# Spreading the latent convolution's blocks among the context's taps in the second half, with one load of its taps a block ahead and four output tiles for the scan

## The chip, the cores and the metric

One core of one Trainium2 chip runs the whole program. The metric is the device time of one execution in microseconds (us), the median of several runs; lower is better.

## The reference: what is computed

One layer of a hybrid backbone runs over two groups of tokens: 256 context tokens and 2048 latent tokens (a grid of 32 rows and 64 columns), 1024 channels wide.

```python
h = rms_norm(x, g_pre) * (1 + scale) + shift
z, xbc, dt_raw, ga, gb, gsil = split(h @ w_in)          # 5664 columns
y_ssd  = bidirectional chunked scan of silu(conv5(xbc)), dt_raw  # chunks of 128 tokens
y_conf = silu(layer_norm(depthwise_conv31(ga * sigmoid(gb)))) * silu(gsil)
out = concat(y_ssd * silu(z), y_conf) @ w_out
return x + gate * rms_norm(out, g_post)                  # and the final states of the context
```

`depthwise_conv31` has 31 taps for each channel. For the context it runs along the 256 tokens; for the latent tokens it runs down the 32 rows of the grid, for each column apart. Those two convolutions are what the change moves about.

## The kernel before, in words

All matrix products are made in pairs of rounded and remainder parts: a weight is split into `wh` and `wl`, the input into `hh` and `hl`, and a product is three matmuls (`wh*hh`, `wh*hl`, `wl*hh`; lines 461 to 463). The tokens are 18 tiles of 128; the first half of the program takes the projections of 10 tiles, the second half (token blocks 3 and 4, 512 tokens each) those of the other 8. The split weights of the first half are kept in DRAM, and the second half loads them again (`load_w`, lines 418 and 419: 512 KB for `wh`, 512 KB for `wl`, three buffers each, asked for three units ahead by `next_w`).

After its `xbc` columns the second half runs through `post(1, 5)`: eight `gab_unit` (each 96 matmuls of 128x512: `gb` and `ga` for two token blocks), then eight `silu_unit` for `z` (48 matmuls each), then those for `gsil`. Into this stream, line by line, `interleave` sets the side work as `merge` counts it out:

- **The scan of tiles 9 to 17** (`scan`, `pass_a`, line 730). A tile loads its inputs `xT` (one buffer) and `bc`, and eight `lb` tiles, rows of running sums spread over all partitions (line 746, issued by ScalarE's queue). GpSimd masks an `lb` (line 758), ScalarE takes its exponential (766), VectorE combines the two directions (770, 771), and TensorE multiplies (`py` 802, `po` 809, `pst` 815 to 817). `skip` (line 836) begins the output tile `yg` from `xT`, and `close` (841) ends it and stores it to `yp`. `yg` has two buffers.
- **The extra work** (line 1061): four context convolutions (`ctx_conv`, line 668: 31 steps on VectorE in 13 pieces) and eight latent convolutions (`lat_conv`, line 701: 6 pieces each), one for each 128 channels, in the order lat, ctx, lat, lat, ctx, lat, and so on: a latent convolution stands right after another, or 13 pieces after it.

A latent convolution is 256 small matmuls (32x64, line 718) of a matrix of taps `kt` with the inputs `cx`. `lat_load` (line 691) brings both in: four loads of 128 KB for the taps `kd` (line 698: 32 partitions each, overlapping stretches of the padded taps) and four of 256 KB for `cx` (line 699: 1024 pieces of 256 bytes each). ScalarE reverses `kd` into `kt` (line 707); from then on `kd` is free. The results pass through two banks of PSUM at a time; VectorE brings them into `cvv` (line 722; one buffer), and four transfers store them (line 727, again in pieces of 256 bytes). `kd` and `cx` have two buffers, `kt` one. A convolution asks for the next one's loads when the next one's inputs are complete (`gl_done`); if not, the next one loads them itself at its own beginning.

All transfers but the `lb` go through the queue of SyncE (SP), which takes them strictly in order: one that has to wait for its buffer or its data holds all behind it. The builder gives each transfer of SP and ScalarE one of eight completion counters in turn, so that a transfer also waits for the one that had this counter last. The PSUM has three banks for the projections (`mm`) and five in turn for all else (`ss`): scan and convolutions share those five.

The order in which each engine takes its instructions is not that of the text. A scheduler in the builder sorts them by a timeline of its own (last lines of the file), so a change of the text moves instructions on every engine. Line numbers below are of this kernel; behind line 692 they are up to 7 higher in the changed one.

Of the kernel before, what the change touches and what calls it, by code (L numbers as in the profile page):

```python
# [8 lines left out]
F32 = mybir.dt.float32  # L9
# [8 lines left out]
P = 128  # L18
# [30 lines left out]
def merge(a, na, b, nb):  # L49

    steps, x, y = [], 0, 0
    for _ in range(na + nb):
        if y * na >= x * nb and x < na or y >= nb:
            steps.append(a)
            x += 1
        else:
            steps.append(b)
            y += 1
    return steps


def take(gen, n):
    for _ in range(n):
        yield next(gen, None)
# [20 lines left out]
def backbone_kernel(ctx, tc, xa, xt_in, cols, rows, wconv, conf_b, gp_row, bg_row, state0, w_mod, w_dt, w_in, w_out,  # L85
# [3 lines left out]
    V, S, T, DMA = (InOrder(tc, e) for e in (nc.vector, nc.scalar, nc.tensor, nc.sync))  # L89
# [30 lines left out]
    def place(i):  # L120

        return (0, i) if i < HT[0] else (1, i - HT[0])
# [66 lines left out]
    pa = ph_a.enter_context(tc.tile_pool(name="pa", bufs=1))  # L189
# [423 lines left out]
    def gab_unit(half, j, hb):  # L613
        wb = next_w()
        wa = next_w()
        gl_done.discard(j)
        for b in ORDER[half]:
            BN, o = BNS[b], TOK[b]
            pg = bank("mm", f"gb{half}_{j}_{b}")
            yield from mm_cm(pg, wb, hb[b])  # L620
            th = ev(f"gth{half}_{j}_{b}")[:, :BN]
            S.activation(th, pg[:, :BN], AF.Tanh, scale=0.5)
            pa_ = bank("mm", f"ga{half}_{j}_{b}")
            yield from mm_cm(pa_, wa, hb[b])
            V.scalar_tensor_tensor(th, th, 1.0, pa_[:, :BN], ADD, MUL)
            DMA.dma_start(GL[j][:, o:o + BN], th)
        if half:
            gl_done.add(j)

    def silu_unit(half, c0, dst, j, hb, order=None):  # L630
        w = next_w()
        for b in order or ORDER[half]:
            BN, o = BNS[b], TOK[b] - half * HT[0] * P
            ps = bank("mm", f"sp{half}_{c0}_{j}_{b}")
            yield from mm_cm(ps, w, hb[b])
            th = ev(f"sth{half}_{c0}_{j}_{b}")[:, :BN]
            S.activation(th, ps[:, :BN], AF.Tanh, scale=0.5)  # L637
            V.scalar_tensor_tensor(th, th, 1.0, ps[:, :BN], ADD, MUL)  # L638
            DMA.dma_start(dst[half][j * P:(j + 1) * P, o:o + BN], th)


    def gate_rows():
        acc = [slab(f"gacc{a}") for a in range(2)]
        for k in range(KT):
            wg = big(f"wg{k}")
            DMA.dma_start(wg, w_mod[k * P:(k + 1) * P, 2 * D:3 * D])
            for a in range(2):
                if k == 0:
                    V.here("tensor_scalar", acc[a][:, :D], wg, sc[:, a, 0:1], None, MUL)
                else:  # L650
                    V.here("scalar_tensor_tensor", acc[a][:, :D], wg, sc[:, a, k:k + 1], acc[a][:, :D], MUL, ADD)
            yield
        br = [slab("bgr0")[0:1, :D], slab("bgr1")[0:1, :D]]
        DMA.dma_start(br[0], bg_row)
        DMA.dma_start(br[1], gp_row)
        for a in range(2):
            for n in range(2):
                ps = bank("ss", f"gp{a}{n}")
                cs = slice(n * 512, (n + 1) * 512)
                T.matmul(ps[0:1, :], ones[:, 0:1], acc[a][:, cs], start=True, stop=True)  # L660
                o = big(f"gr{a}{n}")[0:1, :512]
                V.tensor_tensor(o, ps[0:1, :], br[0][:, cs], ADD)
                V.tensor_tensor(o, o, br[1][:, cs], MUL)
                DMA.dma_start(GGD[a:a + 1, cs], o)
        yield


    def ctx_conv(j, tile):
        g = tile(f"cg{j}")
        G.memset(g[:, 0:15], 0.0)  # L670
        G.memset(g[:, 271:286], 0.0)
        DMA.dma_start(g[:, 15:271], GL[j][:, 0:256])
        yield
        acc = g[:, 512:768]
        w0 = C_CONFW + j * CW
        V.here("tensor_scalar", acc, g[:, 0:256], cv[:, w0:w0 + 1], cfb2[:, j:j + 1], MUL, ADD)
        for t in range(1, CW):
            V.here("scalar_tensor_tensor", acc, g[:, t:t + 256], cv[:, w0 + t:w0 + t + 1], acc, MUL, ADD)
            if t % 3 == 0:
                yield  # L680
        o = g[:, 768:1024]
        S.mul(o, acc, 0.5)
        DMA.dma_start(CV[j * P:(j + 1) * P, 0:256], o)
        yield
# [6 lines left out]
    def lat_load(j, lp):  # L691
        kd = lp.tile([P, 32, 32], F32, tag="kd", name=f"kd{j}", bufs=2)
        x = lp.tile([P, 32, 64], F32, tag="cx", name=f"cx{j}", bufs=2)
        lat_in[j] = kd, x
        for a in range(4):
            rs = slice(a * 32, (a + 1) * 32)
            src = bass.AP(tensor=wconv.tensor, offset=(j * 4 + a) * 64 * 32, ap=[[32, 32], [1, 1024]])
            DMA.dma_start(kd[rs].rearrange("p r g -> p (r g)"), src)
            DMA.dma_start(x[rs], GL[j][:, 256:].rearrange("(g a) (r w) -> a r g w", a=4, w=64)[a])

    def lat_conv(j, lp, cbb, more):
# [28 lines left out]
    def pass_a(i):  # L730
        half, il = place(i)
# [102 lines left out]
        yg = {}  # L834

        def skip(g):
            yg[g] = pa.tile([P, 4, P], F32, tag="yg", name=f"yg{i}{g}", bufs=2)
            V.tensor_tensor(yg[g], xT[:, 4 * g:4 * g + 4, :],
                            cv[:, C_D + 4 * g:C_D + 4 * g + 4].unsqueeze(2).to_broadcast([P, 4, P]), MUL)

# [35 lines left out]
        decay(0, 1)  # L876
        mask(1, 0)
        skip(0)
        load_lb(1, 1)
        yield  # L880
# [37 lines left out]
    def scan(tiles):  # L918

        gens = [pass_a(i) for i in tiles]  # L920
        live, t = [], 0
        while gens or live:
            if gens and t % 7 == 0:
                live.append(gens.pop(0))
            for g in list(live):
                if next(g, 0) == 0:
                    live.remove(g)
            t += 1
            yield


    def interleave(blocks, side, n):
        done = 0
        total = len(side)
        for a, _ in enumerate(blocks):
            want = min(total, -(-total * (a + 1) // n))
            while done < want:
                next(side[done], None)
                done += 1
        while done < total:  # L940
            next(side[done], None)
            done += 1

    def chain(gens):
        for g in gens:
            yield from g

    def run(gen):
        for _ in gen:
            pass  # L950

    def post(half, nb):
        return chain([gab_unit(half, j, hb) for j in range(8)] + [silu_unit(half, Z0, ZS, j, hb) for j in range(8)]
                     + [silu_unit(half, GS0, GS, j, hb) for j in range(nb)])
# [76 lines left out]
    extra = chain([gate_rows()] + [ctx_conv(j, big) for j in range(4)])  # L1031
# [21 lines left out]
    lp = ph_l.enter_context(tc.tile_pool(name="lp", bufs=1, side="right"))  # L1053
# [4 lines left out]
    blocks = post(1, 5)  # L1058
    cg = lambda name: lp.tile([P, D], F32, tag="cg", name=name, bufs=2)
    lat = lambda j: lat_conv(j, lp, cbb, gl_done.__contains__)  # L1060
    extra = chain(f for j in range(4) for f in (lat(2 * j), ctx_conv(j + 4, cg), lat(2 * j + 1)))
    sc_ = scan(range(9, NT))
    run(take(blocks, 24))
    interleave(take(blocks, 24), [sc_] * 4, 24)
    interleave(take(blocks, 344), merge(sc_, 63, extra, 8 * 6 + 4 * 13), 344)
    run(sc_)
    run(extra)
    ph_l.close()
# [107 lines left out]
    def norms(i, yz, nq):  # L1176

        pm = bank("ss", f"pm{i}")
        src = [(c, e, t[1]) for c, e, t in ((0, 4.0 * EPS, yz), (1, EPS, nq)) if t]
        for c, e, t in src:  # L1180
            T.matmul(pm[:, c:c + 1], t, ones[:, 0:1], start=True, stop=True)
        rs = []
        for c, e, t in src:
            ms = p1.tile([P, 1], F32, tag=f"ms{c}", name=f"yms{i}{c}", bufs=2)
            V.tensor_scalar(ms, pm[:, c:c + 1], 1.0 / D, e, MUL, ADD)
            rs.append((c, rstd_of(p1, ms, f"yr{i}{c}")))
        return rs
# [116 lines left out]
    i = order[0]  # L1304
# [21 lines left out]
    for b in range(2):  # L1326
        for m, u in enumerate(last):
            run(take(u, 8))
            if b == 0 and m == 1:
                rs = norms(i, yz, None)  # L1330
# [18 lines left out]
            if b == 1 and m == 0:  # L1349
                rs = norms(i, None, nq)  # L1350
                nq = conf_sqsum(i1, vv[1][0])
            if b == 1 and m == 1:
                n, v = nn[0], vv[0][0]
# [3 lines left out]
            if b == 1 and m == 2:  # L1357
                gs0, v0, n = gs_load(i), v, nn[1]
# [17 lines left out]
    i, nxt, nx2 = order[:3]  # L1376
    banks(i)
    out_part(pso[i], yh, 0, 1)
    rs = norms(nxt, yz, nq)
# [42 lines left out]
    n, n2 = n2, conf_load(order[3])  # L1422
    yh = yhn

    for a, i in enumerate(order[1:], 1):
# [7 lines left out]
        rs = None if last else norms(nxt, yz, nq)  # L1433
# [46 lines left out]
        if a + 3 < NT:  # L1480
            ssd_load(order[a + 3])
            n, n2 = n2, conf_load(order[a + 3])
        else:
            n = n2
# [72 lines left out]
```

## Time and profile before

| What | us |
|---|---|
| Median of 3 runs (1851.51 to 1853.14) | 1852.8 |
| The profiled execution's own time | 1855.05 |
| its span, first to last instruction | 1853.3 |
| TensorE matmul busy in the span | 1793.9 |
| VectorE / ScalarE / GpSimd busy | 1216.5 / 867.1 / 172.2 |
| Mean granted TensorE clock | 0.987 |

The profiled execution took 1.75 us more than its span, and 2.25 us more than the median. The stage with the scan of tiles 9 to 17 and the extra work lies between about 910 and 1300 us. In a table by windows each row gives a stretch, its length, and for each engine the busy time and the count of instructions, then the granted TensorE clock (1.00 is full), the busy share of the 16 DMA engines, and GB/s. In a timeline each row gives the start, the duration (of a merged group: from its first start to its last end), engine, line, operation and tile, and in brackets how long the engine had been idle and what ended that. "SPq" and "ACTq" are the queues that issue transfers.

### The profile page before, as it was taken

The numbers are of one execution on the slowest core, as the hardware profiler recorded it, in microseconds if no ns is written. First come the engines' busy times: TensorE is split into PE (matmuls) and PEld (weight loads), VectorE is DVE, ScalarE is ACT, GpSimd is POOL, SyncE is SP. The second block draws the span as 40 slices with busy tenths as digits, with TensorE's granted clock in tenths as the row PEclk, the third lists the DMA queues.
The fourth block names the chain that finished last, engine by engine and source line by source line (L and its number), as shares of the span: only waits on it lengthen the run. The fifth ranks groups of instructions, "written<-read, shape, count | busy, mean of one in ns | idle before, by whom it ended". The sixth has DMA issues, their size and how long they took to land.

```text
span 1853.3 us, 29884 instructions
## 1 busy us (share of the span) xinstructions
PE 1793.9 (97%) x11167; PEld 1480.5 (80%) x11167; DVE 1216.5 (66%) x1847; ACT 867.1 (47%) x1960; POOL 172.2 (9%) x281
## 2 busy tenths in 40 slices
PE   5999999999999999999999889999999999999998
PEld 2888887888888888888877667777787888888886
DVE  4597857575666762687457375868347878777763
ACT  4747424444455431744235344554245545454441
POOL 1002001011111000100002011110000101111110
PEclk9999999999999999999999889999999999999999
DMA  9656566554786654545697889694977666656632
GB/s 334 215 198 238 204 212 212 190 201 162 261 267 216 222 182 145 178 170 201 195 207 225 176 239 233 229 236 176 290 223 238 194 184 167 172 171 170 185 103 80
DMA packets 304429, 375.22 MB, mean 202 GB/s; under 512 B 84246, under 2 KB 203670, under 8 KB 304284
## 3 DMA queue, kind: packets, MB, share of 16 engines
q1 hardware_dynamic: 283548, 335.56, 58.1%
q10 hardware_dynamic: 20736, 37.76, 7.3%
q8 instruction: 88, 1.44, 0.3%
q14 instruction: 57, 0.47, 0.1%
HBM read 243.66 MB, written 129.59 MB: 201 GB/s over the span
## 4 chain that ended last, share of the span: by engine, by line
PE 87%; DMA 8%; issue 1%; ACT 1%; DVE 1%; SPq 1%; POOL 0%; ACTq 0%; POOLq 0%; DVEq 0%
PE op L81 21%; PE sp L461 6%; PE sp L462 6%; PE sp L463 6%; PE xp L462 5%; PE xp L461 5%; PE xp L463 5%; PE ga L461 3%; PE ga L463 3%; PE ga L462 3%; PE gb L461 3%; PE gb L463 3%; PE gb L462 3%; DMA lb<-lt 3%; PE py L802 2%; PE po L809 2%
## 5 line engine op out<-in xcount | busy, mean ns | idle before, releaser
L766 ACT ACTIVATE lb<-lb,WB 128x128 f32<-128x128 f32 x576 | 184.5, 391 | 162.7 <-POOL lb L758 156.6
L461 PE MATMUL sp<-hh,wh 128*128 128x512 f32 (+1 forms) x640 | 240.0, 375 | 0.0
L463 PE MATMUL sp<-hh,wl 128*128 128x512 f32 (+1 forms) x640 | 237.1, 371 | 0.0
L462 PE MATMUL sp<-hl,wh 128*128 128x512 f32 (+1 forms) x640 | 237.0, 370 | 0.0
L758 POOL TENSOR_SCALAR_AFFINE_SELECT lb<-lb 128x512 f32<-128x512 f32 x144 | 109.1, 761 | 729.9 <-ACT el L755 400.5
L463 PE MATMUL xp<-hh,wl 128*128 128x512 f32 (+1 forms) x456 | 168.0, 368 | 0.0
L462 PE MATMUL xp<-hl,wh 128*128 128x512 f32 (+1 forms) x456 | 167.8, 368 | 0.0
L461 PE MATMUL xp<-hh,wh 128*128 128x512 f32 (+1 forms) x456 | 167.0, 367 | 0.0
L558 DVE SCALAR_TENSOR_TENSOR cva<-raw,cwh,cva 128x1280 f32<-128x1280 f32 (+1 forms) x96 | 141.9, 1487 | 20.4 <-ACT cva L552 18.2
L463 PEld LDWEIGHTS sp<-hh,wl 128*128 128x128 f32 x640 | 121.3, 189 | 21.1
L461 PEld LDWEIGHTS sp<-hh,wh 128*128 128x128 f32 x640 | 121.6, 190 | 20.7 <-issue 0.2
L462 PEld LDWEIGHTS sp<-hl,wh 128*128 128x128 f32 x640 | 121.6, 190 | 20.0
L461 PE MATMUL ga<-hh,wh 128*128 128x512 f32 (+1 forms) x320 | 121.3, 379 | 6.4 <-DMA wh<-whd 5.5
L75 DVE SCALAR_TENSOR_TENSOR cg<-cg,cv 128x256 f32<-128x256 f32 x240 | 123.0, 512 | 3.3
L461 PE MATMUL gb<-hh,wh 128*128 128x512 f32 (+1 forms) x320 | 120.5, 376 | 0.0
L463 PE MATMUL ga<-hh,wl 128*128 128x512 f32 (+1 forms) x320 | 119.2, 373 | 0.5 <-DMA wl<-wld 0.5
L462 PE MATMUL ga<-hl,wh 128*128 128x512 f32 (+1 forms) x320 | 119.4, 373 | 0.0
L463 PE MATMUL gb<-hh,wl 128*128 128x512 f32 (+1 forms) x320 | 119.0, 372 | 0.0
L462 PE MATMUL gb<-hl,wh 128*128 128x512 f32 (+1 forms) x320 | 118.9, 371 | 0.0
L770 DVE TENSOR_TENSOR lb<-lb,lb 128x512 f32<-128x512 f32 x72 | 50.8, 706 | 90.0 <-ACT lb L766 71.7
L638 DVE SCALAR_TENSOR_TENSOR sth<-sth,sp 128x512 f32<-128x512 f32 (+1 forms) x80 | 50.4, 630 | 75.6 <-ACT sth L637 70.7
L755 ACT ACTIVATE el<-lb 64x256 f32<-64x256 f32 x136 | 56.3, 414 | 88.8 <-DMA lb<-lt 71.2
(273 smaller groups left out, 3832.9 us busy)
## 6 DMA issues: line engine op xcount, KB each, us to landing
lb<-lt ACTq DMA_DIRECT2D x144, 256.0 KB, 4.6
wr<-in_w_in SPq DMA_DIRECT2D x88, 256.0 KB, 4.9
whd<-wh SPq DMA_DIRECT2D x44, 512.0 KB, 3.4
wld<-wl SPq DMA_DIRECT2D x44, 512.0 KB, 5.2
wh<-whd SPq DMA_DIRECT2D x44, 512.0 KB, 5.5
wl<-wld SPq DMA_DIRECT2D x44, 512.0 KB, 5.9
xT<-xb SPq DMA_DIRECT2D x18, 512.0 KB, 4.2
yp<-yg SPq DMA_DIRECT2D x36, 256.0 KB, 4.9
```

The costliest lines, as they stand in the source:

```text
L75: return self._tc.keep_in_program_order(getattr(self._eng, name)(*a, **k))
L81: return lambda *a, **k: self._tc.keep_in_program_order(f(*a, **k))
L461: T.matmul(ps[:, :BN], wh[:, k, :], hh[:, k, :], start=(k == 0), stop=False)
L462: T.matmul(ps[:, :BN], wh[:, k, :], hl[:, k, :], start=False, stop=False)
L463: T.matmul(ps[:, :BN], wl[:, k, :], hh[:, k, :], start=False, stop=(k == KT - 1))
L558: V.scalar_tensor_tensor(a[:, :n], raw[:, t:t + n], cwh[:, ct * 5 + t:ct * 5 + t + 1], a[:, :n], MUL, ADD)
L638: V.scalar_tensor_tensor(th, th, 1.0, ps[:, :BN], ADD, MUL)
L755: S.activation(el[g][rs, q:q + 2, :], E[g, hq, 0][rs, j::2, :], AF.Exp)
L758: G.affine_select(E[g, hq, d], E[g, hq, d], pattern=[[0, 4], [sg, P]], compare_op=ALU.is_ge, fill=NEG, base=0, channel_multiplier=-sg)
L766: S.activation(lb[:, h, :], lb[:, h, :], AF.Exp, bias=WB[:, i, c + h:c + h + 1])
L770: V.tensor_tensor(a, a, E[g, hq, 1], ADD)
L802: T.matmul(py[g][j * HD:(j + 1) * HD, q * P:(q + 1) * P], xt[g][:, h * HD:(h + 1) * HD], E[g, hq, 0][:, t, :], start=True, stop=True)
```

## The change

Three things change, all in the second half.

1. **Order of the extra work.** Each context convolution is cut into 7 and 6 pieces, and after each stands one latent convolution: ctx 7, lat, ctx 6, lat. Ahead of all stands one piece that loads the first latent convolution's inputs; the pieces to be merged with the scan are one more.
2. **The taps.** The four loads of `kd` become one with three dimensions on the source's side (4 groups, 32 offsets, 1024 values).
3. **The scan's output tiles.** For tiles of the second half (10 to 17) `yg` comes from the pool of the second half, `lp`, with four buffers; tile 9 keeps the two of `pa`.

```diff
@@ lat_load
+        src = bass.AP(tensor=wconv.tensor, offset=j * 4 * 64 * 32, ap=[[64 * 32, 4], [32, 32], [1, 1024]])
+        DMA.dma_start(kd.rearrange("p r g -> p (r g)"), src)
         for a in range(4):
             rs = slice(a * 32, (a + 1) * 32)
-            src = bass.AP(tensor=wconv.tensor, offset=(j * 4 + a) * 64 * 32, ap=[[32, 32], [1, 1024]])
-            DMA.dma_start(kd[rs].rearrange("p r g -> p (r g)"), src)
             DMA.dma_start(x[rs], GL[j][:, 256:].rearrange("(g a) (r w) -> a r g w", a=4, w=64)[a])
@@ pass_a, skip
-            yg[g] = pa.tile([P, 4, P], F32, tag="yg", name=f"yg{i}{g}", bufs=2)
+            pool, n = (lp, 4) if half else (pa, 2)
+            yg[g] = pool.tile([P, 4, P], F32, tag="yg", name=f"yg{i}{g}", bufs=n)
@@
+    def run_once(f):
+        f()
+        yield
@@ second half
-    extra = chain(f for j in range(4) for f in (lat(2 * j), ctx_conv(j + 4, cg), lat(2 * j + 1)))
+    ctxs = [ctx_conv(j + 4, cg) for j in range(4)]
+    extra = chain([run_once(lambda: lat_load(0, lp))]
+                  + [f for j in range(4) for f in (take(ctxs[j], 7), lat(2 * j), take(ctxs[j], 6), lat(2 * j + 1))])
...
-    interleave(take(blocks, 344), merge(sc_, 63, extra, 8 * 6 + 4 * 13), 344)
+    interleave(take(blocks, 344), merge(sc_, 63, extra, 1 + 8 * 6 + 4 * 13), 344)
```

What the scheduler makes of it is seen at three places.

**SP's queue, around the load of the taps of convolution 4** (`kd4`; `cv` is a store of `cvv`, `wh4256`/`wl4256` are `gb`'s weights of unit 5, `wh3232`/`wl3232` are `ga`'s of unit 5, `cx3` are inputs, `yp`, `st` and `gl` stores). Before:

```order
L698 DMA kd4_10488<-in_wconv 32x1024
L727 DMA cv_78<-cvv1_9400 32x32x64 x2
L418 DMA wh4256_1_9642<-whd25_145 128x1024
L419 DMA wl4256_1_9641<-wld25_189 128x1024
L626 DMA gl3_71<-gth1_3_4_9512 128x512
L727 DMA cv_78<-cvv1_9400 32x32x64 x2
L698 DMA kd4_10488<-in_wconv 32x1024 x3
L699 DMA cx3_9706<-gl3_71 32x32x64 x4
L846 DMA yp11_90<-yg110_9630 128x512
L832 DMA st11_108<-sb110_9965 128x512
L626 DMA gl4_72<-gth1_4_3_9718 128x512
L698 DMA kd5_10795<-in_wconv 32x1024
```

and right behind these:

```order
L727 DMA cv_78<-cvv2_9760 32x32x64 x4
L698 DMA kd5_10795<-in_wconv 32x1024
L735 DMA bc13_10312<-xb1_64 128x4x128
L698 DMA kd5_10795<-in_wconv 32x1024 x2
L418 DMA wh3232_1_9646<-whd17_137 128x1024
L419 DMA wl3232_1_9645<-wld17_181 128x1024
```

Now, from `wh4256` to `wh3232`:

```order
L418 DMA wh4256_1_9567<-whd25_145 128x1024
L419 DMA wl4256_1_9566<-wld25_189 128x1024
L626 DMA gl3_71<-gth1_3_4_9427 128x512
L699 DMA cx3_10018<-gl3_71 32x32x64 x3
L727 DMA cv_78<-cvv1_9451 32x32x64 x4
L699 DMA cx3_10018<-gl3_71 32x32x64
L696 DMA kd4_10535<-in_wconv 128x1x1024
L847 DMA yp11_90<-yg110_9550 128x512
L832 DMA st11_108<-sb110_9817 128x512
L626 DMA gl4_72<-gth1_4_3_9693 128x512
L735 DMA bc13_10290<-xb1_64 128x4x128
L418 DMA wh3232_1_9571<-whd17_137 128x1024
```

Between the two weights' `wl4256` and `wh3232` stood 22 transfers, among them six of two convolutions' stores and seven of two convolutions' taps; now there are 14, with four stores and one load of taps. `kd4`, which waits until ScalarE has reversed `kd2`, stood ahead of the stores of `cvv1` and now stands behind them.

**VectorE, where tile 11's output tiles `yg110` and `yg111` are begun** (`lb` line 770 is the sum of the two directions, lines 821 to 825 carry the state on, 843 and 845 end tile 10's `yg`). Before:

```order
L770 TENSOR_TENSOR lb11000_9313<-lb11000_9313,lb11001_9315 128x512
L770 TENSOR_TENSOR lb11010_9390<-lb11010_9390,lb11011_9392 128x512
L821 TENSOR_TENSOR Sf1_260<-Sf1_260,eTf_252 128x512
L823 TENSOR_TENSOR yo101_9369<-po101_9298,el101_8880 128x512
L825 TENSOR_TENSOR Sf1_260<-Sf1_260,pst1010_9303 128x512
L838 TENSOR_TENSOR yg110_9630<-xT11_9258,cv_214 128x512
L625 SCALAR_TENSOR_TENSOR gth1_3_3_9267<-gth1_3_3_9267,ga1_3_3_9269 128x512
L843 TENSOR_TENSOR yg101_9156<-yg101_9156,py101_9293 128x512
L845 TENSOR_TENSOR yg101_9156<-yg101_9156,yo101_9369 128x512
L770 TENSOR_TENSOR lb11100_9508<-lb11100_9508,lb11101_9510 128x512
L838 TENSOR_TENSOR yg111_9685<-xT11_9258,cv_214 128x512
```

Now:

```order
L791 TENSOR_TENSOR xw1001_9130<-xt100_8900,WS_258 128x512
L839 TENSOR_TENSOR yg110_9550<-xT11_9271,cv_214 128x512
L839 TENSOR_TENSOR yg111_9677<-xT11_9271,cv_214 128x512
L770 TENSOR_TENSOR lb10110_9042<-lb10110_9042,lb10111_9044 128x512
L793 TENSOR_TENSOR xwl1001_9132<-xw1001_9130,xwh1001_9131 128x512
L722 SCALAR_TENSOR_TENSOR cvv0_8933<-cp0_0_8934,cbb_8306 128x8x64
```

Both are begun in the middle of tile 10 instead of at its end, far ahead of tile 10's own `yg101`.

**TensorE, where `ga` of unit 6 begins** (`wh3360` and `wl3360` are its weights, `cp3` the banks of convolution 3). Before:

```order
L718 MATMUL cp3_0_10505<-cx3_9706,kt3_10486 32x64
L718 MATMUL cp3_1_10506<-cx3_9706,kt3_10486 32x64
L461 MATMUL ga1_6_3_10573<-hh3_7102,wh3360_1_10111 128x512
L462 MATMUL ga1_6_3_10573<-hl3_7103,wh3360_1_10111 128x512
L463 MATMUL ga1_6_3_10573<-hh3_7102,wl3360_1_10110 128x512
```

Now:

```order
L718 MATMUL cp3_0_10584<-cx3_10018,kt3_10533 32x64
L718 MATMUL cp3_1_10585<-cx3_10018,kt3_10533 32x64
L461 MATMUL ga1_6_3_10482<-hh3_7102,wh3360_1_9961 128x512
L462 MATMUL ga1_6_3_10482<-hl3_7103,wh3360_1_9961 128x512
L461 MATMUL gb1_6_4_10576<-hh4_7312,wh4384_1_9957 128x512
L462 MATMUL gb1_6_4_10576<-hl4_7313,wh4384_1_9957 128x512
L463 MATMUL gb1_6_4_10576<-hh4_7312,wl4384_1_9956 128x512
```

The last three rows come once more, and only then the third matmul of `ga1_6_3`, the first that needs `wl3360`: six matmuls of the next token block now stand ahead of it, and all but the first two small matmuls of convolution 3 stand behind all of `ga1_6_3`.

Counted in projection matmuls on TensorE, the distance from one latent convolution's first matmul to the next one's was 183, 63, 183, 66, 183, 63, 183, and is now 120, 132, 96, 162, 120, 138, 120.

## The prediction

> **What bounds the kernel now.** I read the page first, for the engine that carries the span.
>
> ```profile
> span 1853.3 us, 29884 instructions
> PE 1793.9 (97%) x11167; PEld 1480.5 (80%) x11167; DVE 1216.5 (66%) x1847; ACT 867.1 (47%) x1960; POOL 172.2 (9%) x281
> ```
>
> TensorE's matmuls fill 97% of the span; no other engine is near that. A change that takes no matmul away can only win where TensorE idles or runs at a lower clock. The table by windows says where that is.
>
> ```profile
> 850.00:900.00 50.00, 50.00 (x222) 41.40 (x221) 38.39 (x30) 17.79 (x19) 0.30 (x3) 1.00 0.55 179
> 950.00:1000.00 50.00, 45.94 (x253) 36.48 (x252) 35.56 (x65) 22.82 (x62) 7.03 (x11) 1.00 0.99 238
> 1000.00:1050.00 50.00, 43.61 (x687) 33.79 (x685) 22.10 (x35) 21.20 (x56) 7.77 (x9) 0.90 0.76 186
> 1050.00:1100.00 50.00, 41.34 (x202) 32.37 (x203) 35.65 (x65) 22.18 (x55) 5.34 (x8) 0.90 0.82 209
> 1100.00:1150.00 50.00, 48.58 (x725) 38.46 (x724) 29.45 (x47) 26.55 (x65) 6.95 (x12) 0.97 0.88 243
> 1150.00:1200.00 50.00, 47.24 (x349) 37.49 (x348) 40.46 (x74) 27.14 (x73) 8.37 (x10) 0.93 0.73 221
> 1200.00:1250.00 50.00, 47.40 (x602) 37.41 (x601) 33.73 (x53) 26.34 (x62) 6.31 (x9) 0.93 0.93 240
> 1250.00:1300.00 50.00, 50.00 (x504) 39.55 (x504) 40.66 (x72) 19.41 (x45) 3.06 (x4) 1.00 0.50 173
> ```
>
> Before and behind the stage TensorE is busy 50.00 of 50.00 at clock 1.00. In the six windows between it idles 4.06 + 6.39 + 8.66 + 1.42 + 2.76 + 2.60 = 25.9 us. Where it works there, the granted clock is lower: busy time times the missing share is 43.61 x 0.10 + 41.34 x 0.10 + 48.58 x 0.03 + 47.24 x 0.07 + 47.40 x 0.07 = 16.6 us. So each idle microsecond costs 16.6 / 25.9 = 0.64 us of clock besides, and 42.5 us is the most that this change can win. The next view is TensorE's waits in that stretch.
>
> ```profile
> PE ga L461 <- DMA wh<-whd: 5.5, 1, 5.5
> PE px L778 <- issue: 5.3, 2, 4.1
> PE cp L718 <- DVE cvv L722: 4.4, 1, 4.4
> PE pst L815 <- DVE cvv L722: 3.5, 1, 3.5
> PE cp L718 <- issue: 2.6, 1, 2.6
> PE pst L815 <- ACT xwh L792: 1.7, 1, 1.7
> PE cp L718 <- ACT sb L831: 1.4, 1, 1.4
> PE px L778 <- PE pb L855: 0.7, 1, 0.7
> PE ga L463 <- DMA wl<-wld: 0.5, 1, 0.5
> PE pst L816 <- DVE xwl L793: 0.4, 1, 0.4
> ```
>
> Two groups. The convolutions' own (`cp`, `pst` behind `cvv`) and the late weights: 5.5 + 4.4 + 3.5 + 2.6 + 1.4 + 0.5 = 17.9 us. The scan's: 5.3 + 1.7 + 0.7 + 0.4 = 8.1 us. How the first group arises is seen in SP's queue, in order of time.
>
> ```profile
> 1021.68 0.34 SPq L698 DMA_DIRECT2D kd<-in_wconv  x1
> 1022.11 0.98 SPq L727 DMA_DIRECT2D cv<-cvv  x2
> 1023.19 1.41 SPq L418 DMA_DIRECT2D wh<-whd  x1
> 1026.67 2.38 SPq L727 DMA_DIRECT2D cv<-cvv  x2
> 1029.09 4.31 SPq L698 DMA_DIRECT2D kd<-in_wconv  x3
> 1033.51 5.32 SPq L699 DMA_DIRECT2D cx<-gl  x4
> ...
> 1053.74 5.39 SPq L727 DMA_DIRECT2D cv<-cvv  x4
> 1062.58 0.37 SPq L418 DMA_DIRECT2D wh<-whd  x1
> ```
>
> The queue sat still until 1021.68, since `kd4` waits for ScalarE to free `kd2`; the stores of `cvv1` stood behind it. Other engines then:
>
> ```profile
> 1030.15 0.33 ACTq L746 DMA_DIRECT2D lb<-lt  x1
> 1030.59 0.62 ACT L792 CAST xwh<-xw 128x512 fp32r<-128x512 f32 x1 [8.52 <-DMA wh<-whd]
> 1034.89 1.29 DVE L722 SCALAR_TENSOR_TENSOR cvv<-cp,cbb 128x512 f32<-128x512 f32 x2 [2.22 <-DMA kd<-in_wconv]
> ```
>
> ScalarE stood for 8.52 us ahead of an `lb` load whose completion counter was still held by the `wh` issued at 1023.19; VectorE could not write `cvv2` before 1034.89, when the late stores of `cvv1` (one buffer) had left it. That is the 4.4. Its followers came late (3.5), and the next pile of taps and stores put `ga`'s weights behind it (5.5).
>
> ```profile
> SPq L698 <- ACT kt L707: 24.2, 2, 14.7
> SPq L733 <- DVE yg L838: 19.1, 5, 6.4
> DVE yg L838 <- DMA yp<-yg: 10.6, 4, 4.2
> ```
>
> These rows sum SP's and VectorE's waits in the stage: 24.2 us for freed taps (once 14.7, the one above), 19.1 us because `xT` waits for `skip`, which itself waited 10.6 us for stores of `yg`. The last view is what transfers take, issue to landing: the first five rows in the stage, the sixth in the first half's scan.
>
> ```profile
> lb<-lt ACTq DMA_DIRECT2D x60, 256.0 KB, 5.2
> wh<-whd SPq DMA_DIRECT2D x21, 512.0 KB, 7.0
> cv<-cvv SPq DMA_DIRECT2D x31, 256.0 KB, 5.3
> xT<-xb SPq DMA_DIRECT2D x8, 512.0 KB, 5.6
> kd<-in_wconv SPq DMA_DIRECT2D x24, 128.0 KB, 4.5
> ...
> lb<-lt ACTq DMA_DIRECT2D x29, 256.0 KB, 4.3
> ```
>
> **The change part by part.** *Spreading.* No matmul, vector step or byte is added or taken. One projection matmul takes 50.00 / 222 = 0.225 us, so the distance between convolutions that were close was 63 x 0.225 = 14.2 us, and is at least 96 x 0.225 = 21.6 us now (scan work not counted). In 14.2 us had to fit: matmuls, VectorE, four stores (5.39 us of issue, 5.3 us to land), and the next convolution's first write of `cvv`. In 21.6 us it fits, and `kd4` has gone behind the stores of `cvv1`, so the 14.7 us wait delays nothing that TensorE asks for next. Ahead of `wh3232` 14 transfers are left of 22. All six waits of the first group hang on this; I let four fifths of the 17.9 go, 14.3 us, and keep a fifth because the bytes stay and the five shared banks still mix scan and convolutions. Bounds: 7.9 (only the two behind `cvv`, 4.4 and 3.5) and 17.9.
>
> *One load of taps for four.* 24 issues fewer in SP's queue: three of them took 4.31 us at 1029.09, when the queue was full. It gains nothing by itself where the queue has slack, and frees three completion counters for each convolution. Its landing is not in this trace: at best as a `wh` of the same 512 KB, 7.0 us; at worst as four quarters one after the other, 4 x 4.5 = 18.0 us. For the convolution either is hidden by 21.6 us of lead. I take 7.0, the row of the same size, and no gain or loss of its own.
> [...]
>
> *Four output tiles.* VectorE's 10.6 us of waits for `yp` and SP's 19.1 us behind them end. What is late next is `xT`: `yg110` is begun soon behind its load, up to 5.6 us of wait for VectorE, hidden because the tile's products come more than 33 projection matmuls (7.4 us) later. This, and fewer counters held, helps the second group; but `px` and `pst` also wait for `lb` tiles, which keep their place, so I let half of 8.1 go, 4.0 us. Bounds: 0 and 8.1.
>
> *What comes new.* The order itself shows `wl3360` late: six matmuls were set ahead of the third of `ga1_6_3`. The scheduler's idea of a transfer knows no full queue, so I expect a wait there, between 0 and the 6.0 (5.5 + 0.5) that the like took before. Since `kd5`, two `cx4` and four stores still stand ahead of `wh3360`, I take 4.0. The first load now precedes the first convolution by a whole block; that is ahead of the first of the quoted windows with a loss, so I take it at nothing.
>
> *The end.* Behind 1250 TensorE is full, so what is saved passes on whole. Convolution 7 now ends 36 matmuls (8.1 us) later; DMA has room there (0.50), and its stores are wanted far later.
>
> *Sum.* Idle: 14.3 + 4.0 - 4.0 = 14.3 us; with clock 14.3 x 1.64 = 23.4 us. The profiled execution took 1855.05, so it would take 1831.6; the median stands 2.25 below it: 1852.8 - 23.4 = 1829.4 us.
>
> [...]
>
> **The rivals.**
> *A, slower: the whole load of taps clogs the queue.* If it lands in 18.0 instead of 7.0 us and what is queued behind it waits along, weights come up to 11.0 us late. `ga`'s weights can be asked for only 48 matmuls (10.8 us) ahead of their need and take 7.0, a slack of 3.8, with scan work somewhat more. Units 3 to 7 each have a load of taps in front: five waits of 6.0, as measured, are 30.0 us, with clock 49.2, against 30.0 (18.3 x 1.64) won: 1852.8 + 19.2 = 1872. It decides from 3.7 us late for each unit on (30.0 / 1.64 / 5). For it: `kd` loads hold counters, and one late weight cost 5.5. Against: in the new order `kd4` stands four rows ahead of `wh3232`, but is issued some 11 us before `wh3232` may be. [...] Chance 0.09.
> *B, little won: the transfers bound the stage.* The bytes are the same: shares 0.99 to 0.93 in the six windows make 255.5 us of 300; in 276.6 us that is 0.92, and at 0.99 TensorE idled 4.06 in 50. `lb` tiles land in 5.2 here against 4.3 in the first half. Then half of the first group, all of the second and a wait of 6.0 stay: (8.95 - 6.0) x 1.64 = 4.8 us won, 1848. Against: from 1100 to 1150 the share was 0.88 with 1.42 idle. Chance 0.20.
> *C, all won*: no wait is left and none is new: 1852.8 - 42.5 = 1810.3. For it: before 900 and behind 1250 TensorE shows what it does when nothing is late. Against: all six waits and the scan's would have to go at once. Chance 0.12 for over 33 us.
> *D, nothing:* the scheduler could sort the text's order away. The distances counted in its order say that it did not; but gain and new waits may cancel. Chance 0.08.
>
> **How the numbers follow.** The forecast, 12 to 33 us won, has 0.51. A measurement of this kernel tells about 0.2%, 3.7 us, from no change. Faster: 0.51 + 0.12 + 0.20 = 0.83; same 0.08 (D); slower 0.09 (A). The range leaves out A, D and the ends of B and C: 1811 (C, nearly all won) to 1849 (B).
>
> **What would show it.** Right: the six windows' idle time near 11 us instead of 25.9 and clocks of 0.95 and over; no `cp` waiting for `cvv`, no `yg` for `yp`, and no long wait of SP for `kt` ahead of `cv`; one wait of `ga` for `wl`. `kd`'s landing, 7 or 18 us, decides on the taps. Wrong: `ga` waiting for weights in several units (A), `lb` landing later than 5.2 and POOL waiting for it as before (B), or the same waits moved behind 1250, where TensorE was full.

## The result, and the profile after

The changed kernel takes 1886.1 us (median of 4 runs, 1881.97 to 1889.72) where the kernel before took 1852.2 on the same chip. The ratio on record is 1.0169, with a 95% interval of 1.0147 to 1.0192; the two medians alone, 34.0 us apart, give 1.018, inside that interval. It is slower by 1.7%; forecast were 1829.4 us and a win. The profiled execution's page begins so:

```profile
span 1881.1 us, 29870 instructions
PE 1802.6 (96%) x11167; PEld 1487.0 (79%) x11167; DVE 1215.6 (65%) x1847; ACT 866.5 (46%) x1960; POOL 168.3 (9%) x281
```

VectorE, ScalarE and GpSimd do the same work in the same time. The span of the profiled execution is 27.8 us longer. The table by windows of the stage, of the changed kernel:

```profile
900.00:950.00 50.00, 48.24 (x238) 39.09 (x236) 17.75 (x32) 8.29 (x12) 0.24 (x4) 1.00 0.63 170
950.00:1000.00 50.00, 42.48 (x450) 33.69 (x450) 31.77 (x53) 21.73 (x54) 5.80 (x8) 0.92 0.70 181
1000.00:1050.00 50.00, 45.84 (x458) 36.26 (x458) 31.15 (x54) 22.55 (x56) 7.39 (x10) 0.91 0.94 238
1050.00:1100.00 50.00, 43.04 (x452) 33.67 (x451) 34.05 (x60) 24.80 (x64) 7.53 (x10) 0.93 0.78 199
1100.00:1150.00 50.00, 45.41 (x474) 35.53 (x473) 27.64 (x46) 22.54 (x56) 6.45 (x11) 0.93 0.88 217
1150.00:1200.00 50.00, 40.47 (x425) 31.40 (x423) 28.89 (x51) 22.57 (x58) 5.32 (x8) 0.90 0.67 191
1200.00:1250.00 50.00, 42.55 (x462) 33.52 (x461) 28.27 (x47) 21.17 (x58) 5.22 (x8) 0.97 0.82 208
1250.00:1300.00 50.00, 44.54 (x455) 35.39 (x456) 36.53 (x65) 27.00 (x67) 6.97 (x9) 0.90 0.72 212
```

and of the kernel before the one row that the prediction did not show:

```profile
900.00:950.00 50.00, 49.49 (x481) 40.27 (x480) 20.22 (x32) 13.61 (x21) 1.09 (x5) 1.00 0.80 203
```

From 900 to 1300 TensorE now idles 400 - 352.6 = 47.4 us, before 0.5 + 25.9 = 26.4: 21.0 more. The missing clock times the busy time is 23.5 us, before 16.6: 6.9 more. Together 27.9, so that these 400 us account for the whole of the longer span. The DMA engines are no busier: a mean share of 0.77 in these eight rows, 0.80 before. TensorE's waits in the stage, of the changed kernel (waited for; us in total, times, longest):

```profile
PE cp L718 <- DVE cvv L722: 10.9, 3, 5.6
PE pst L815 <- DVE yo L823: 7.4, 2, 4.8
PE px L778 <- DVE cvv L722: 5.3, 1, 5.3
PE pst L815 <- ACT xwh L792: 5.3, 1, 5.3
PE ga L461 <- DMA wh<-whd: 4.4, 1, 4.4
PE cp L718 <- ACT sb L831: 4.2, 1, 4.2
PE po L809 <- DVE yo L823: 4.0, 1, 4.0
```

Late weights are one of these seven largest rows. VectorE (`yo`) and ScalarE (`xwh`) were late themselves; three of the four long waits for them lead back to these rows:

```profile
949.56 1.29 DVE L839 TENSOR_TENSOR yg<-xT,cv 128x512 f32<-128x512 f32 x2 [11.27 <-DMA xT<-xb]
998.68 0.62 ACT L792 CAST xwh<-xw 128x512 fp32r<-128x512 f32 x1 [9.82 <-DMA kd<-in_wconv]
1221.74 0.84 ACT L755 ACTIVATE el<-lb 64x256 f32<-64x256 f32 x2 [11.93 <-DMA zs<-sth]
```

In the last two rows ScalarE needs neither taps nor `zs`: ahead of each stands an `lb` load that waits for a completion counter which `kd`, and the `zs` queued behind another `kd`, still held. VectorE's `xT` of the first row was issued late, because in SP's queue `cx` stood ahead of it and waited for a store of `gl` behind a load of taps:

```profile
SPq L699 <- DMA gl<-gth: 6.6, 1, 6.6
```

The chain of waits, of the changed kernel, shows how long transfers take beside a load of taps (start, duration, what):

```profile
988.88 9.28 DMA kd<-in_wconv
...
1099.74 14.69 DMA wh<-whd
...
1206.06 15.24 DMA zs<-sth
```

Around the second of these, SP's queue in the changed kernel:

```profile
1098.11 0.54 SPq L696 DMA_DIRECT2D kd<-in_wconv  x1
1098.76 0.42 SPq L847 DMA_DIRECT2D yp<-yg  x1
1099.27 0.38 SPq L832 DMA_DIRECT2D st<-sb  x1
1099.74 0.54 SPq L418 DMA_DIRECT2D wh<-whd  x1
1100.37 0.60 SPq L419 DMA_DIRECT2D wl<-wld  x1
```

Nothing was held in the queue: five issues in 2.9 us. But the trace also has the time of each step of the completion counters, and there the five read (steps, and when they came):

```
kd  issued 1098.11:  1 step at 1099.07;              4 steps 1109.87 to 1111.49
yp  issued 1098.76: 12 steps 1101.38 to 1102.69;     4 steps 1110.84 to 1112.55
st  issued 1099.27: 12 steps 1102.02 to 1103.14;     4 steps 1111.28 to 1113.18
wh  issued 1099.74: 12 steps 1104.40 to 1105.89;     4 steps 1112.51 to 1114.42
wl  issued 1100.37: 12 steps 1107.10 to 1108.17;     4 steps 1113.82 to 1115.73
```

`kd`'s last step comes 13.4 us after the issue. Of each transfer behind it 12 of the 16 steps have come after 4 to 8 us; the last of the other four comes only after `kd`'s last. Twelve of the sixteen steps of `wh` had come at 1105.89; TensorE stood until 1114.47 for the rest. All eight loads of taps have one step 1.0 to 2.2 us after the issue and then four, the last of them 9.3 to 17.5 us after it. In the kernel before, each of the 32 loads of taps has 16 steps, the last 2.4 to 7.5 us after the issue. Those have 32 as the slowest dimension of both sides, the one load has 4 and 128. No trace here shows the DMA engines one by one: that a late step stands for one of the sixteen engines, and that the one load so runs on four of them, is my reading of these steps.

How many transfers come late can be counted from the same steps. Of those issued from 900 to 1300, the last step came more than 10 us after the issue for these (in brackets how late, us):

```
      before             changed
wh    1 of 23 (10.2)     5 of 21 (12.0 to 14.7)
wl    1 of 23 (10.4)     5 of 21 (13.1 to 15.4)
yp    none of 17         4 of 16 (11.8 to 13.8)
xT    none of 8          1 of 8  (16.1)
```

The rest changed little: the median `wh` needed 5.7 us before and 6.4 now. The table of issues is no help here, since its medians rest on the few transfers for which it has a landing, such as 7 of 23 `wh` before and 2 of 21 now.

### The profile page after: what moved, and what is told of

Same layout as the page of the kernel before. It is cut to its first block, busy times and chain, and to the rows that moved or that the text cites. A ratio compares the mean times of both kernels' runs of the same rounds, so it can differ in the third digit from the quotient of the medians.

```text
span 1881.1 us, 29870 instructions
## 1 busy us (share of the span) xinstructions
PE 1802.6 (96%) x11167; PEld 1487.0 (79%) x11167; DVE 1215.6 (65%) x1847; ACT 866.5 (46%) x1960; POOL 168.3 (9%) x281
## 4 chain that ended last, share of the span: by engine, by line
PE 83%; DMA 10%; DVE 2%; issue 2%; ACT 1%; SPq 1%; POOL 1%; ACTq 0%; POOLq 0%; DVEq 0%
PE op L81 20%; PE sp L461 7%; PE sp L462 6%; PE sp L463 6%; PE xp L462 5%; PE xp L461 5%; PE xp L463 5%; DMA lb<-lt 5%; PE gb L461 3%; PE ga L461 3%; PE gb L463 3%; PE gb L462 3%; PE ga L462 3%; PE ga L463 3%; PE py L802 2%
## 5 line engine op out<-in xcount | busy, mean ns | idle before, releaser
L461 PEld LDWEIGHTS xp<-hh,wh 128*128 128x128 f32 x456 | 86.0, 189 | 14.1
```

What stands on the lines that cost most here:

```text
L461: T.matmul(ps[:, :BN], wh[:, k, :], hh[:, k, :], start=(k == 0), stop=False)
```

## The experiments

Two things were to be explained: the loss, and why the 23.4 us of the forecast were not there beside it. For the loss, theory E, by the reading above: the one load occupies four engines, and all that is queued behind it ends when these do. Against it, theory O (the new order puts things late) and I (one large transfer is slow by itself). Each ratio below is to the kernel before on the same chip; where two changed versions are compared, it is by these ratios.

**e1, four loads again.** The changed kernel with the taps as before:

```diff
-        src = bass.AP(tensor=wconv.tensor, offset=j * 4 * 64 * 32, ap=[[64 * 32, 4], [32, 32], [1, 1024]])
-        DMA.dma_start(kd.rearrange("p r g -> p (r g)"), src)
         for a in range(4):
             rs = slice(a * 32, (a + 1) * 32)
+            src = bass.AP(tensor=wconv.tensor, offset=(j * 4 + a) * 64 * 32, ap=[[32, 32], [1, 1024]])
+            DMA.dma_start(kd[rs].rearrange("p r g -> p (r g)"), src)
```

> The changed kernel with the taps loaded by four transfers of 128 KB again; the order of the blocks and the four output tiles stay. Theory E (the one load runs on four of the sixteen DMA engines, so that each transfer behind it ends when these four do): the loss goes and the rest of the change shows its own worth, by the blind sum 1829 us, at any rate under 1845; completions of the transfers behind kd no longer come as 12 early and 4 late. Theory O (the new order itself puts things late, the one load only adds to it): 1860 us or more, with the waits of TensorE for cvv and pst still there.

Ratio to before 1.0000 (0.9981 to 1.0019). The loss is gone, but no gain has come: theory E holds for the loss, and the forecast for the rest does not. The counters agree: of the `wh` issued at 1095.48, among four loads of taps, all 16 steps come between 1099.02 and 1100.67. TensorE's waits of this kernel, which has the changed one's order, begin with

```profile
PE cp L718 <- DVE cvv L722: 11.1, 3, 5.7
```

and have no row for `yo`, `xwh` or `wh`. So what the one load added to TensorE's waits is mainly `yo` (7.4 + 4.0), `xwh` (5.3) and `wh` (4.4), 21.1 us; the waits for `cvv` were there without it.

**e2, one load alone.** The opposite edit, put into the kernel before.

> The kernel before with one change: the taps in one load. Theory E: slower by about as much as the whole change or more, 1880 to 1910 us, since the load stands close ahead of weights and stores there too. Theory O: within 10 us of the kernel before, 1843 to 1863.

1.0181 (1.0162 to 1.0201), 33 us slower with the old order and the old output tiles. Theory O falls: the one load alone makes the whole loss. The largest waits of TensorE in it:

```profile
PE ga L461 <- DMA wh<-whd: 10.1, 1, 10.1
PE cp L718 <- DMA cx<-gl: 9.3, 2, 8.4
PE px L778 <- issue: 7.9, 2, 5.7
PE px L778 <- DVE cvv L722: 7.7, 1, 7.7
```

**e6, one load with 128 rows.** As the changed kernel, but the input array of the taps holds the overlapping stretches written out (4 MB), so that the load has 128 rows on both sides:

```diff
-        src = bass.AP(tensor=wconv.tensor, offset=j * 4 * 64 * 32, ap=[[64 * 32, 4], [32, 32], [1, 1024]])
-        DMA.dma_start(kd.rearrange("p r g -> p (r g)"), src)
+        DMA.dma_start(kd.rearrange("p r g -> p (r g)"), wconv[j])
...
-        "wconv": wconv,
+        "wconv": np.stack([np.stack([wconv[j, p // 32, p % 32:p % 32 + 32].reshape(1024) for p in range(128)]) for j in range(8)]),
```

> The changed kernel with one load of taps per convolution, of the same 512 KB into the same places, but read from an image in DRAM in which the overlapping stretches stand written out (128 rows of 1024), so that its slowest dimension on both sides is 128 instead of 4 and 128. Theory E (the loss comes from the four engines): its completion counter steps 16 times instead of once and 4 times, and the time is that of the version with four loads, 1848 to 1862 us. Theory I (the loss comes from one large load in the place of four small ones, whatever engines carry it): 1875 us or more.

0.9946 (0.9928 to 0.9964): 10 us faster than before, 2.2% faster than the changed kernel, with as many transfers of the same size. Theory I falls. The counter of each load now takes 16 steps, the last of them 4.1 to 7.4 us after the issue over all eight loads (in the changed kernel 9.3 to 17.5), and no `wh`, `wl`, `yp` or `xT` of the stage takes over 10 us any more.

**e7, two loads with two rows each.** The changed kernel with the load halved:

```diff
-        src = bass.AP(tensor=wconv.tensor, offset=j * 4 * 64 * 32, ap=[[64 * 32, 4], [32, 32], [1, 1024]])
-        DMA.dma_start(kd.rearrange("p r g -> p (r g)"), src)
+        for b in range(2):
+            src = bass.AP(tensor=wconv.tensor, offset=(j * 4 + 2 * b) * 64 * 32, ap=[[64 * 32, 2], [32, 32], [1, 1024]])
+            DMA.dma_start(kd[b * 64:(b + 1) * 64].rearrange("p r g -> p (r g)"), src)
```

> The changed kernel with the taps in two loads of 64 partitions each, whose slowest dimension on the source's side is 2. Theory E: each load runs on two engines, both on the same two, so these carry 256 KB each for a convolution where four carried 128 KB each; the taps and all that is queued behind them land about twice as late (some 20 to 30 us after the issue instead of 9 to 16), and the time goes up by as much again or more: 1910 to 1960 us. Theory I: two smaller loads are no worse than one, 1870 to 1888 us.

1.0360 (1.0338 to 1.0381), 67 us slower: twice the loss, for twice the bytes on each engine if a late step stands for an engine. The counter of each of the two loads issued from 1125.08 on steps once early and twice late. Those of the transfers behind (`st`, `wh`, `wl`, `yp`) step 14 times early and twice late, the late steps at 1142.65 to 1146.96. E holds: the loss goes where the taps have no four late steps (e1, e6), comes with the one load alone (e2) and doubles where the late steps are two (e7).

**e3, the new order alone**, with four loads and two output tiles (the diff's other two parts taken back).

> The kernel before with the new order of the blocks and nothing else (four loads of taps, two output tiles). By the blind sum the spreading alone wins (14.3 - 4.0) x 1.64 = 16.9 us: 1836 us. Theory E: 1825 to 1850. Theory O: 1860 or more.

1.0019 (0.9999 to 1.0039): nothing won, perhaps 3.5 us lost. TensorE's waits in the stage:

```profile
PE cp L718 <- DVE cvv L722: 10.4, 3, 5.5
PE px L778 <- issue: 6.8, 2, 4.9
PE px L778 <- DVE cvv L722: 4.7, 1, 4.7
```

The waits of `ga` for weights (5.5 + 0.5) and of `pst` for `cvv` (3.5) are gone, as forecast. The wait of `cp` for `cvv` has grown from 4.4 to 10.4, and `px` now waits for `cvv` too.

**e5, four output tiles alone.**

```diff
-            yg[g] = pa.tile([P, 4, P], F32, tag="yg", name=f"yg{i}{g}", bufs=2)
+            pool, n = (lp, 4) if half else (pa, 2)
+            yg[g] = pool.tile([P, 4, P], F32, tag="yg", name=f"yg{i}{g}", bufs=n)
```

> The kernel before with the four output tiles and nothing else. By the blind sum 4.0 x 1.64 = 6.6 us are won: 1846 us, with VectorE's waits of yg for yp (10.6 us) gone. If the output tiles were part of the loss (theory Y): 1856 or more.

0.9979 (0.9961 to 0.9996): some 4 us, with the 6.6 of the forecast inside the interval (1 to 7 us). VectorE's wait for `yp` is gone, and one for the inputs has come:

```profile
DVE yg L839 <- DMA xT<-xb: 14.3, 4, 9.7
```

The three parts alone, e3, e5 and e2, multiply to 1.0019 x 0.9979 x 1.0181 = 1.0179, and the whole change has 1.0169: they do not hinder or help each other beyond the noise.

What takes the place of the waits in the new order? In e1 TensorE waits three times for over 4 us until VectorE empties a convolution's banks. Ahead of the second (a bank waited for from 1164.97 to 1170.12) VectorE did this:

```profile
1168.77 0.69 DVE L770 TENSOR_TENSOR lb<-lb,lb 128x512 f32<-128x512 f32 x1 [4.91 <-ACT lb L766]
1169.38 1.28 DVE L722 SCALAR_TENSOR_TENSOR cvv<-cp,cbb 128x512 f32<-128x512 f32 x2
```

VectorE stood 4.91 us for the exponentials of an `lb` pair, with the emptying of the banks behind it in its order. The third (4.1 us, to 1229.37) is of the same kind: VectorE stood idle for 2.8 us of it, ahead of an `lb` sum. The first and longest (5.7 us, to 1076.94) is not. There VectorE was at work for all but 0.3 us, with the beginning of the output tiles and pieces of the context convolution ahead of the banks:

```profile
1072.53 1.72 DVE L839 TENSOR_TENSOR yg<-xT,cv 128x512 f32<-128x512 f32 x2
1074.77 1.51 DVE L75 SCALAR_TENSOR_TENSOR cg<-cg,cv 128x256 f32<-128x256 f32 x3
```

So in none of the three do the stores of `cvv` hold the banks; in two it is the scan's `lb` chain (load, mask, exponential), in one VectorE's own order. Theory L: the loads stand too late in the text. Theory B, from the prediction: the DMA engines are full and nothing helps.

**e8 and e9, `lb` loads a step earlier**, in e1 and in the kernel before, for tiles 9 to 17: each `load_lb` in `pass_a` is moved ahead of the `yield` before it.

> The version with four loads of taps (new order, four output tiles), and besides each lb load of the scan's tiles 9 to 17 set one step of the scan earlier in the text. Theory L (VectorE's step that empties the convolution's banks stands in order behind the sum of an lb pair, and that waits for a chain of load, mask and exponential that starts too late): TensorE's waits of cp and px for cvv, 11.1 and 4.1 us, go and the time is 1825 to 1842 us. Theory B (the DMA engines are full in this stage, an earlier load only pushes others back): 1848 to 1862 us.

> The kernel before with the lb loads of tiles 9 to 17 one step earlier and nothing else. Theory L: the scan's waits (8.1 us idle) go, those of the convolutions that stand close together (17.9 us) stay: 8.1 x 1.64 = 13.3 us less, 1838 to 1846 us. Theory B: no change, 1848 to 1860 us, or slower.

0.9988 (0.9973 to 1.0003) and 1.0010 (0.9995 to 1.0025): no change. But the edit hardly reached the chip. Of the 72 `lb` loads of tiles 9 to 17, 64 stand behind just as many of ScalarE's instructions in e8 as in e1, and 66 in e9 as in the kernel before; the others moved by 3 at most. So these runs show that an earlier place in the text does not help, and say nothing of loads that really come earlier, for theory L or for B. A load of direction 0 waits for its place besides: its four places are read by the products `py` of the tile before. That the scheduler puts a load where it believes its place free is my reading of this, not shown.

**e10, more places.** e6, and the last `lb` of direction 0 in tiles 10 to 17 goes into the two `yg` tiles of pool `pa` that only tile 9 still used:

```diff
-                lb = pa.tile([P, 4, P], F32, tag=f"lb{d}", name=f"lb{i}{g}{hq}{d}", bufs=4)
+                if i >= 10 and g == 1 and hq == 1 and d == 0:
+                    lb = pa.tile([P, 4, P], F32, tag="yg", name=f"lb{i}{g}{hq}{d}", bufs=2)
+                else:
+                    lb = pa.tile([P, 4, P], F32, tag=f"lb{d}", name=f"lb{i}{g}{hq}{d}", bufs=4)
```

> The version with one load of taps on sixteen engines (e6), and in tiles 10 to 17 the last lb load of direction 0 goes into the two output tiles that tile 9 left free, so that direction 0 has six places instead of four. Theory L' (a load of lb can't start earlier because its place is still read by the products of the tile before; VectorE then stands at the sum of the pair, and the emptying of the convolution's banks behind it): the waits of cp and px for cvv (8.8 and 5.0 us in e6) halve or go, and the time falls by 6 to 20 us against e6, to 1828 to 1842 us. Theory B (the DMA engines are full): no change against e6, 1844 to 1853 us.

0.9871 (0.9851 to 0.9890): 24 us faster than before, 14 us faster than e6. TensorE's largest waits in the stage, first e6's, then e10's:

```profile
PE cp L717 <- DVE cvv L721: 8.8, 3, 4.7
PE px L777 <- DVE cvv L721: 5.0, 1, 5.0
```

```profile
PE cp L717 <- DVE yg L846: 2.8, 1, 2.8
PE cp L717 <- issue: 1.7, 2, 1.2
PE cp L717 <- DVE cvv L721: 1.5, 2, 1.2
```

Theory B falls: from 900 to 1300 the DMA engines now move 92.1 MB, in e6 87.4, and TensorE idles less. VectorE ahead of the same banks as in e1's second wait, now with 0.91 us of wait where e1 had 4.91:

```profile
1146.19 0.69 DVE L772 TENSOR_TENSOR lb<-lb,lb 128x512 f32<-128x512 f32 x1 [0.91 <-ACT lb L768]
1146.80 1.28 DVE L721 SCALAR_TENSOR_TENSOR cvv<-cp,cbb 128x512 f32<-128x512 f32 x2
```

Here the loads did come sooner: in tiles 11 to 17 all but one of the 56 stand behind fewer of ScalarE's instructions than in e6, half of them by 11 or more. VectorE's step that empties the banks still stands behind as many `lb` sums as in e6, or one more, so it is the sums that came earlier. Why e6's first wait, in which VectorE was at work (3.8 us), shrank to 1.2 us as well is not told apart.

**e11, more places and earlier loads** (e10 with the edit of e8).

> As e10, and besides each lb load of tiles 9 to 17 one step of the scan earlier in the text, as in e8. Theory L': places are now there for an earlier load, so at least as fast as e10: 1825 to 1842 us. Theory B: no change against e6, 1844 to 1853 us, or slower.

0.9851 (0.9830 to 0.9871), 1828.6 us in its own runs: the fastest of all, 28 us under the kernel before. Against e10 the intervals overlap, and 69 of the 72 loads stand where they stood in e10, so the earlier loads are not shown to add anything.

**e12, one load with 128 rows alone**, in the kernel before.

> The kernel before with one load of taps on sixteen engines (from the written-out image) and nothing else. If the gain of e6 over the kernel before (0.5%) comes from the 24 transfers fewer alone: 0.993 to 0.997 of before here too. If it takes the new order or the four output tiles beside it: 0.998 to 1.002.

0.9965 (0.9951 to 0.9978): some 6.5 us for 24 transfers fewer. They were not free, as far as this shows: the edit also changes where the taps stand in DRAM, and no run takes the two apart.

**e13, the old order in e11.**

```diff
-    ctxs = [ctx_conv(j + 4, cg) for j in range(4)]
-    extra = chain([run_once(lambda: lat_load(0, lp))]
-                  + [f for j in range(4) for f in (take(ctxs[j], 7), lat(2 * j), take(ctxs[j], 6), lat(2 * j + 1))])
+    extra = chain(f for j in range(4) for f in (lat(2 * j), ctx_conv(j + 4, cg), lat(2 * j + 1)))
...
-    interleave(take(blocks, 344), merge(sc_, 63, extra, 1 + 8 * 6 + 4 * 13), 344)
+    interleave(take(blocks, 344), merge(sc_, 63, extra, 8 * 6 + 4 * 13), 344)
```

> e11 with the blocks of the extra work in the order of the kernel before (one load of taps on sixteen engines, four output tiles, more places for lb and earlier loads stay). If the spreading is worth something once the lb loads no longer hold VectorE (theory S: both losses end last in turn, and each hides the other's removal): slower than e11 by 6 us or more, 0.988 to 0.995 of the kernel before, with waits of cp for cvv or of ga for wh back. If the spreading is worth nothing at all: 0.983 to 0.987, as e11.

0.9908 (0.9889 to 0.9927), so with the places for `lb` the new order is worth 0.57%, 10.6 us, where alone it was worth nothing. Theory S (each of two losses hides what the other's removal would bring) holds. With the old order the late weights are back:

```profile
PE px L780 <- DVE cvv L721: 5.7, 2, 4.3
PE ga L461 <- DMA wh<-whd: 4.8, 1, 4.8
```

## Why the prediction was wrong, point by point

- **The bound and its price.** The bound was right: what was lost lies in TensorE's idle time and clock between 900 and 1300, and the 42.5 us held as a ceiling (28 us won in e11). The factor of 0.64 was too high for this kernel: 23.5 / 47.4 = 0.50 on all idle time, 6.9 / 21.0 = 0.33 on what was added. The clock records of the two traces show why: from 930 to 1300 the clock is halved in stretches of 3.41 or 6.83 us each, 7 of them before (37.6 us in all, each begun within a wait of 1.4 to 5.5 us or at most 1.6 us behind it) and 10 in the changed kernel (54.6 us, each within a wait of 1.6 to 5.6 us or at most 0.5 us behind it). So 21.0 us more of idle time brought three more stretches: here the price went by the number of such stretches and not by the length of the waits.
- **One load of taps.** The step that failed is "no gain or loss of its own". The landing of 7.0 was too low (9.3 to 17.5; all eight lie within the bounds of 7.0 and 18.0), but the error lay in what I asked of it: "for the convolution either is hidden by 21.6 us of lead". It is; TensorE never waited for taps. The cost fell on what was queued behind, in other engines' work: `xT`, `yp`, `wh`, `zs`, and the `lb` loads by their counters. It was measured at 33 us (e2). I followed a late landing to the convolution's own need and, as rival A, to weights alone.
- **Rival A** had the sign and the place, at 1872 against 1886. Its path was one of several: five late weights were priced, one came (4.4), and the rest of what the load added were waits for `yo` and `xwh` (16.7), 14.1 of them behind `xT`, `kd` and `zs` as shown above. I put "issued some 11 us before" against it; but a `kd` needed 9.3 to 17.5 us, so that a lead of 11 us need not clear it.
- **Spreading.** The forecast was 14.3 us of idle time; alone it was worth nothing (e3), beside more `lb` places 10.6 us of time (e13). The step that failed is "in 21.6 us it fits": I counted matmuls, VectorE's steps and stores, and gave VectorE as free to empty the banks. In e1 it stood ahead of an `lb` sum in two of the three long waits and was at work on other steps in the longest; with e10's places 1.5 us of such waits of `cp` are left. The sign stood in the kernel before: of the 3.5 us in which `pst` waited for `cvv`, put down to late stores, VectorE stood idle ahead of an `lb` sum for 2.1 us. The waits for weights and of `pst` for `cvv` did go.
- **Four output tiles.** Right in sign and kind, some 4 us where 6.6 were forecast. `xT` is what became late next, as said.
- **The new wait for `wl3360`**, 4.0 us, did not come: no row of `ga` for `wl` in the changed kernel. What the scheduler puts ahead of a load that it takes for late is no proof of a wait.
- **24 issues fewer** were put at nothing; with the load of 128 rows e12 gains 6.5 us.
- **Rival B** (the transfers bound the stage) is refuted by e10: DMA had room; places for `lb` were short. **Rival D**, that gain and new waits cancel, at a chance of 0.08, is what the order alone did (e3), and the order with the output tiles (e1).

## What to carry to other kernels

Before several loads are merged into one, look at the slowest dimension that is left: with four large rows this load took up to 17.5 us, and four of the sixteen steps of transfers queued behind it came as late, though the merged load itself had time; alone it cost 33 us (e2). With 128 rows the same bytes took at most 7.4 us (e6). A hidden landing says nothing of what stands behind it; ask who is next in the queue and whose counter it holds. When one of two stalls is removed and the time stays, look at what the freed engine does next in order, and take the other away too before the first is judged.

## What the runs showed of the hardware

A load with 4 as its slowest dimension held back four of the sixteen counter steps of each of the four transfers issued right behind it by some 8 to 10 us (table of steps above); with 2 as the slowest dimension of each of two loads the same bytes cost 67 us instead of some 31 (e7 against the changed kernel). The share of busy DMA engines hides it, since it is a mean over all sixteen (0.77 in the changed kernel, 0.80 before). A counter that steps 12 or 14 times early and 4 or 2 times late is how it was seen. Halved clock stood behind short waits too: in the kernel before, 3.41 us of it begin at 1109.11, behind a wait of 1.42 us, and 6.83 us at 1180.79, behind one of 1.68 us. In e10 the window from 1150 has no wait of TensorE over 2.8 us (its list above) and 3.0 us of idle time in all, at a clock of 0.96; by the clock record 6.83 us at half clock begin at 1196.15, just behind that wait.

```profile
1150.00:1200.00 50.00, 47.00 (x481) 37.21 (x481) 33.56 (x55) 28.04 (x71) 8.82 (x11) 0.96 0.82 234
```
